# A Mamba-2 and gMLP layer on one core: the order of the first stage, two late factors, the projection weight's slots, and the last rows of the output

## The chip, the cores and the metric

The kernel runs on one core of a Trainium2 chip. The metric is the device time of one execution in microseconds (us). The core has a matrix engine (TensorE, PE in the profile; its weight loads are PEld), a vector engine (VectorE, DVE), a scalar engine (ScalarE, ACT), GpSimd (POOL) and a sync engine (SP) that here only issues loads. Each engine works through its own list of instructions in order, and semaphores make one wait for another.

## The reference

One layer, 1024 rows (time) of 1024 features, everything in fp32. Cut to what matters here:

```python
mod = silu(c) @ ada_w + ada_b
shift, scale, gate = split(mod, 3)
h = rms_norm(x, norm_w) * (1 + scale) + shift
proj = h @ w_in                 # gm_u, gm_v, gm_z, ssm_z, xbc, dt, g_a, g_b
y_a = spatial_gating(gelu(gm_u), gelu(gm_v), ...) * silu(gm_z)
y_b = rms_norm((ssd_scan(silu(conv(xbc)), dt, ...) + d_skip * xs) * silu(ssm_z), groups of 256)
merged = sigmoid(g_a) * (y_a @ w_proj_a) + sigmoid(g_b) * (y_b @ w_proj_b)
out = rms_norm(x + gate * (merged @ w_out), final_norm_w)
```

## The kernel before, in words

**Arithmetic.** A product of fp32 matrices is made of three matmuls on rounded parts: high x high, high x low, low x high. Each operand is split into them: ACT casts the high part (a CAST), DVE subtracts it to get the low part. Large products go by a Strassen scheme with seven products of half-size blocks. The normed and modulated input h is kept transposed as four blocks b11, b12, b21, b22 and their sums t1 to t4, each in four row tiles k and in a high and a low part (`b11h0`, `b11l0`, ...). One `product` is 12 matmuls of 128x512; after each one `run_tasks` moves a counter of slots on by one and runs what `later(delay, f)` has put off until that slot.

**Who sets the order.** Instructions under `pin` keep the order of the program among themselves. All others are placed by the framework's scheduler, which works with its own estimates of durations, so a task's slot decides only from when on it can be placed. Loads go to SP's queue (`load`), stores to ACT's (`store`), both in order with what else stands on the engine.

**First stage (0 to 72 us).** x is loaded in eight tiles xt[0..7]. `square(t)` sums the squares of a tile on ACT, `factors` makes the inverse root (a power on POOL), `normed` scales half a tile. Then h is made for eight blocks of 128 features in the order `KS = (0, 4, 1, 5, 2, 6, 3, 7)`; n counts the steps in this order. For step n: `matvec(n)` multiplies silu(c) with the two column blocks aw[n] of ada_w and copies the result to row; `modulation(n)` turns it to a column by two small matmuls, and two small DVE operations make md (scale and shift); `transposes(n, h)` turns half h of the rows on PE into px; `rows_of_h(n, h)` reads px with md: ACT writes the high part and an fp32 copy hf, DVE subtracts for the low part. `first_products(n)` then makes 12 matmuls of h with 256 columns of w_in (w0, split by `split_w0`) into accs, six for each half; the loop counts them with `at`, and at given counts inserts what prepares step n + 1 (`prepare`), the sums t1 to t4 (`t_first` to `t_parts`, `last_sums`) and the four matmuls of `dt_products`. `warm` issues small matmuls without use of their result. The first `vx` matmul begins the next stage.

**Pairs (148 to 920 us).** The columns of w_in in pairs of 128-column blocks, seven products each. Accumulators x and y take turns, and are emptied by ACT copies or DVE adds (`c1x`, `c2x` and so on, line 552). Beside them, from the 17th pair on, `wb_load(i)` loads each of 16 half blocks (wbr) of the second projection weight, `wb_quarter(i)` casts the fourth quadrant (wba), `wb_sums(i)` makes the sums and casts the first two parts (wbb0), and after more slots the last two (wbb2). wbr, wba and wbb have one buffer each, so a cast waits for the store of what stood there before, and a load for the last reader.

**Projection by w_proj_b (1180 to 1327 us).** Units (product name, k); in the first ones, named p1, `post2` and `post3` of the last two SSD groups are inserted: the inverse roots of their rows are turned on PE (`y3p`) and stored.

**Output (1327 to 1402 us).** Seven products by w_out in four row tiles each, added to rows of x (`collect`). The last one (a12) completes rows 0 to 3: the square of each half row is summed on ACT, `root` makes the factor, `finish` applies it and fnw (final_norm_w) and issues the store of the row. Row 3 is done in two column halves, and its factor by three Newton steps on DVE (`inv_root`).

Of the kernel before, what the change touches and what calls it, by code (L numbers as in the profile page):

```python
# [16 lines left out]
P = 128  # L17
# [4 lines left out]
NG = 8  # L22
# [13 lines left out]
def hybrid_kernel(  # L36
# [131 lines left out]
    with tc.tile_pool(name="p0", bufs=1, reuse_waits="tile") as p0:  # L168
# [65 lines left out]
        load(wd, w_in[:, COL_DT : COL_DT + NH].rearrange("(k p) c -> p k c", p=P))  # L234
        at = 0
        for src, n in [(conv_b, 32), (ssm_norm_w, 16), (gm_ln_w, 8), (gm_ln_b, 8)]:
            load(pkb[at : at + n, 0], src[0].rearrange("(r q) -> r q", q=P))
            at += n
        load(pkb[:, 1], conv_w[0].rearrange("k (i q) -> (k i) q", q=P))

        def warm(n):

            for _ in range(n):
                mm(accs[1][1][:, 0:P], ident, ones)
# [10 lines left out]
        def matvec(n):  # L255
# [7 lines left out]
            pin(V.tensor_copy(row, pm[:, 0:256]) if n == 0 else A.copy(row, pm[:, 0:256]))  # L263
# [94 lines left out]
        def halves(n):  # L358

            return (0, 1) if KS[n] < 4 else (1, 0)  # L360
# [8 lines left out]
        def factors(b):  # L369
            bs = slice(4 * b, 4 * b + 4)  # L370
# [10 lines left out]
        for t in range(4):  # L381
            square(t)
        factors(0)
        for t in range(4):
            normed(t, 0, V)
        transposes(0, 0)
        split_w0(0)
        for t in range(4):
            normed(t, 1, V)
        matvec(0)  # L390
        warm(3)
        modulation(0)
        warm(8)
        rows_of_h(0, 0)
        for t in range(4, NCH):
            square(t)
# [1490 lines left out]
```

## Time and profile before

| what | value |
|---|---|
| time, median of 3 runs | 1400.14 us (1397.68 to 1400.6) |
| the profiled execution | 1403.9 us, span of its instructions 1402.1 us |
| mean granted clock of PE | 0.991 |
| PE, DVE, ACT, POOL busy | 98%, 75%, 57%, 16% of the span |
| idle PE time in the span | 1402.1 - 1374.4 = 27.7 us |
| bytes moved | 288.60 MB, 205 GB/s over the span |

Busy shares are means over the stages. A row of the timeline or of the chain gives start, duration, engine, line and `out<-in`; what stands in brackets is the idle time of the engine before it and what ended it. A matmul row's duration reaches from the start of its first to the modelled end of its last. In a row of windows, the eighth item is the granted clock: at 0.50 PE does half its work.

### The profile page before, as it was taken

Reading aid. Unit: us, or ns where it says so; the run is one execution under the profiler, and the core shown is the slowest. Engines: PE = TensorE matmul, PEld = TensorE weight load, DVE = VectorE, ACT = ScalarE, POOL = GpSimd, SP = SyncE. Lnnn points to the kernel's source line nnn. Section 1 sums busy time; section 2 is a strip of 40 time slices with the busy share of each in tenths; the row PEclk is TensorE's granted clock in tenths of the full one; section 3 lists DMA queues with packets and bytes.
Section 4 is the critical chain, followed back from the end, with each engine's and each line's share of the span. In section 5 each row is a group of like instructions: output and inputs, shape, how many; then the busy total and the mean of one; then the engine's idle time right before and its main releaser. Section 6 shows DMA issues by size and latency. Waiting matters only on the chain.

```text
span 1402.1 us, 20253 instructions
## 1 busy us (share of the span) xinstructions
PE 1374.4 (98%) x6971; PEld 1139.7 (81%) x6971; DVE 1045.4 (75%) x1703; ACT 802.2 (57%) x1448; POOL 220.0 (16%) x208
## 2 busy tenths in 40 slices
PE   8999999999999999999999999999999999999997
PEld 6688878888888888887888888888888878888886
DVE  3777766777778889777788686388767755859976
ACT  5764656666566665555676555587766714233443
POOL 0000000000000011200200100027878750000001
PEclk9999999999999999999999999999999999999999
DMA  8675443343334668686675774498777748978913
GB/s 265 191 239 149 120 120 108 110 128 106 131 110 146 200 195 267 210 259 213 191 219 180 226 229 134 160 350 310 279 253 278 272 152 289 333 252 316 379 44 120
DMA packets 247227, 288.60 MB, mean 206 GB/s; under 512 B 14508, under 2 KB 194132, under 8 KB 247124
## 3 DMA queue, kind: packets, MB, share of 16 engines
q1 hardware_dynamic: 173716, 203.76, 45.3%
q10 hardware_dynamic: 73408, 83.54, 17.5%
q8 instruction: 55, 0.90, 0.3%
q14 instruction: 48, 0.39, 0.1%
HBM read 199.79 MB, written 87.46 MB: 205 GB/s over the span
## 4 chain that ended last, share of the span: by engine, by line
PE 77%; DMA 11%; DVE 5%; ACT 2%; issue 2%; POOL 1%; SPq 1%; ACTq 0%; DVEq 0%; POOLq 0%
PE xcb L536 6%; PE xuz L536 6%; PE xz L536 6%; PE xx L536 6%; PE xg L536 5%; PE vx L921 3%; PE yz L536 3%; PE ycb L536 3%; PE yuz L536 3%; PE yx L536 3%; PE yg L536 3%; PE pma L81 3%; DMA dcy<-acs_d 2%; PE ox L1750 2%; PE oy L1750 2%
## 5 line engine op out<-in xcount | busy, mean ns | idle before, releaser
L759 POOL TENSOR_TENSOR wog<-wog,gb 128x256 f32<-128x256 f32 x16 | 23.0, 1454 | 626.4 <-DMA wog<-in_w_out_dram 587.7
L1079 ACT ACTIVATE dcy<-dcy,nacs 128x128 f32<-128x128 f32 x256 | 78.5, 389 | 14.7 <-POOL dcy L1074 14.6
L1074 POOL TENSOR_SCALAR_AFFINE_SELECT dcy<-dcy 128x1024 f32<-128x1024 f32 x32 | 34.9, 1091 | 142.6 <-DMA yl<-ya_d 96.1
L1071 ACT ACTIVATE ea<-dcy 64x512 f32<-64x512 f32 x64 | 40.0, 626 | 14.5 <-DMA dcy<-acs_d 11.9
L81 PE MATMUL pma<-yh,wah 128*128 128x512 f32 x128 | 44.4, 428 | 0.0
L994 ACT ACTIVATE ac<-ac 128x1024 f32<-128x1024 f32 x32 | 33.9, 1061 | 16.4 <-DVE ac L992 16.2
L81 PE MATMUL pma<-yh,wal 128*128 128x512 f32 x128 | 43.0, 417 | 0.0
L1099 DVE TENSOR_TENSOR dcy<-dcy,pc 128x1024 f32<-128x1024 f32 x32 | 39.0, 1218 | 5.1 <-PE pc L84 4.2
L1159 DVE TENSOR_TENSOR ym<-yn,ea 128x512 f32<-128x512 f32 (+1 forms) x32 | 19.9, 623 | 30.2 <-PE yn L81 30.1
L1496 DVE SCALAR_TENSOR_TENSOR yn<-yn,par,rb 128x512 f32<-128x512 f32 x32 | 24.0, 749 | 23.8 <-DMA yn<-yb_d 23.8
L1161 POOL TENSOR_TENSOR yz<-y,sl 128x512 f32<-128x512 f32 x32 | 41.3, 1291 | 1.1
L81 PE MATMUL pma<-yl,wah 128*128 128x512 f32 x128 | 40.9, 402 | 0.0
L1160 POOL TENSOR_TENSOR y<-y,ym 128x512 f32<-128x512 f32 (+1 forms) x32 | 36.5, 1141 | 14.5 <-DVE ym L1159 14.1
L791 ACT CAST wbb<-wbr 128x512 fp32r<-128x512 f32 x32 | 19.8, 619 | 32.6 <-DMA wb_d<-wbb 25.6
L81 PEld LDWEIGHTS yn<-sl,st 128*128 128x128 f32 x224 | 30.5, 191 | 8.5 <-POOL yz L1181 2.3
L81 PE MATMUL sp<-xe,bn 128*128 128x256 f32 x112 | 33.6, 418 | 3.2 <-DVE ssq L1190 1.8
L81 PE MATMUL yn<-sl,st 128*128 128x128 f32 x224 | 31.5, 277 | 5.1 <-DVE st L1129 5.1
L992 DVE SCALAR_TENSOR_TENSOR ac<-c2cb,cwt,ac 128x1023 f32<-128x1023 f32 (+2 forms) x24 | 31.1, 1296 | 6.7 <-ACT ac L990 6.6
L81 PE MATMUL yi<-dcy,xd 128*64 128x128 f32 x512 | 35.4, 281 | 0.1
L992 DVE SCALAR_TENSOR_TENSOR ac<-c2x,cwt,ac 128x1023 f32<-128x1023 f32 (+2 forms) x24 | 30.7, 1280 | 5.9 <-ACT ac L990 5.8
L1765 POOL TENSOR_TENSOR r<-r,fnw 128x512 f32<-128x512 f32 x2 | 2.5, 1293 | 205.9 <-ACT junk L1763 205.9
L1127 POOL TENSOR_TENSOR st<-st,cd 128x256 f32<-128x256 f32 x48 | 32.8, 684 | 10.8 <-PE yn L81 8.2
(2982 smaller groups left out, 4440.4 us busy)
## 6 DMA issues: line engine op xcount, KB each, us to landing
sl<-s_d SPq DMA_DIRECT2D x32, 768.0 KB
s_d<-ac ACTq DMA_DIRECT2D x32, 512.0 KB
wb_d<-wbb ACTq DMA_DIRECT2D x32, 512.0 KB
dcy<-acs_d SPq DMA_DIRECT2D x32, 512.0 KB
av<-in_w_in_dram SPq DMA_DIRECT2D x36, 256.0 KB
aw<-in_ada_w_dram SPq DMA_DIRECT2D x16, 512.0 KB
wbr<-in_w_proj_b_dram SPq DMA_DIRECT2D x32, 256.0 KB
yb_d<-yz ACTq DMA_DIRECT2D x32, 256.0 KB
```

The lines of the kernel that those rows point to most:

```text
L81: pin(PE.matmul(acc, l, r, start=first, stop=last))
L536: pin(PE.matmul(ps, lw[:, k * P : (k + 1) * P], r[k], start=first and n + k == 0, stop=n == 2 and k == 3, skip_group_check=not first))
L921: pin(PE.matmul(ps[pn][j], l[:, j * P : (j + 1) * P], r, start=nm in ("p1", "p5", "p2") and n + units[i][1] == 0, stop=n == 2 and k == 3, ...
L992: V.scalar_tensor_tensor(ac[:, s:], cc[:, : S - s], conv_wt[:, 3 - s, i : i + 1], ac[:, s:], op0=ALU.mult, op1=ALU.add)
L994: A.activation(ac, ac, AF.Silu)
L1071: A.activation(ea[hh * HD : (hh + 1) * HD], dcy.rearrange("p (j e) i l -> p e j (i l)", e=2)[hh * HD : (hh + 1) * HD, hh], AF.Exp)
L1074: G.affine_select(out=d8, in_=d8, compare_op=ALU.is_ge, fill=-1e30, base=0, pattern=[[0, 2 * HPG], [1, P]], channel_multiplier=-1)
L1079: A.activation(dcy[:, h, i, :], dcy[:, h, i, :], AF.Exp, bias=sub[:, i, h : h + 1])
L1099: V.tensor_tensor(d3, d3, pc[:, 0:256].unsqueeze(1).to_broadcast([P, HPG, 256]), op=ALU.mult)
L1160: G.tensor_add(y1[:, :, t0:], y1[:, :, t0:], m[:, :, t0:])
L1161: G.tensor_mul(yz, y1, sl[:, 4:6])
L1750: pin(PE.matmul(ps, a[:, tsl], b[:, cs], start=first and n + j == 0, stop=n == 2 and j == 3, skip_group_check=not first))
```

## The change

Four parts.

1. **First stage.** The factors of a half are made in two steps (three tiles, then one; `squares`). All `normed` are on DVE (two tiles were on ACT), and the copy of row 0 is on ACT. Step 0 is written out by hand: the transposes of step 1's first half go early, the `warm` matmuls are 16 instead of 22 after the first split and go into pd, step 0 is begun with six products, then come matvec(1), the transposes and rows for its second half, modulation(1), and step 1's first half between the remaining products. In `prepare`, matvec stands together with one half's transposes at place 2, and modulation with the other half's at place 7, followed by both `rows_of_h`; before, the four stood at 1, 3, 5 and 9. Some sums and `dt_products` are at later places. The loads of wd and of the small parameters come after those of aw[2] and w0[2].
2. **Weight halves.** Loads come every 9 slots instead of 43 // 5, the quarter 4 slots after the load instead of 2, and the last two parts 2 slots after the first two instead of 3.
3. **Last factors.** The two `post3` are at k = 4 and 6 of p1 instead of 3 and 4.
4. **End.** All instructions of the last product are pinned in a written order. Rows 0 to 3 are each finished in halves: ACT on the high columns (POOL has multiplied those by fnw), DVE on the low ones. Row 3's factor is a power on POOL.

```diff
-            pin(V.tensor_copy(row, pm[:, 0:256]) if n == 0 else A.copy(row, pm[:, 0:256]))
+            pin(A.copy(row, pm[:, 0:256]))
...
-            return (0, 1) if KS[n] < 4 else (1, 0)
+            return (0, 1) if KS[n] < 4 or n == 1 else (1, 0)
...
+        def squares(a, b):
+            for t in range(a, b):
+                square(t)
+            factors(a, b)
+
+        squares(0, 3)
+        squares(3, 4)
+        for half in range(2):
+            for t in range(4):
+                normed(t, half, V)
         transposes(0, 0)
         split_w0(0)
-        for t in range(4):
+        matvec(0)
+        load_aw(2)
+        load_w0(2)
+        late_loads()
+        transposes(1, 0)
+        warm(2)
+        modulation(0)
+        rows_of_h(0, 0)
+        squares(4, 7)
+        for t in (4, 5):
+            normed(t, 0, V)
+        squares(7, 8)
+        for t in (6, 7):
+            normed(t, 0, V)
+        warm(8)
+        start = first_products(0)
+        for _ in range(6):
+            next(start)
+        warm(6)
+        matvec(1)
+        for t in (4, 5):
             normed(t, 1, V)
-        matvec(0)
-        warm(3)
-        modulation(0)
-        warm(8)
-        rows_of_h(0, 0)
-        for t in range(4, NCH):
-            square(t)
-        factors(1)
-        for half in range(2):
-            for t in range(4, NCH):
-                normed(t, half, A if t > 5 else V)
+        transposes(0, 1)
+        modulation(1)
+        rows_of_h(0, 1)
         split_w0(1)
+        for t in (6, 7):
+            normed(t, 1, V)
+        for _ in range(4):
+            next(start)
+        rows_of_h(1, 0)
+        for _ in start:
+            pass
 
         def prepare(n):
 
-            if n == 1:
+            a, b = halves(n)
+            if n == 2:
                 return {
-                    6: lambda: (warm(6), transposes(0, 1), rows_of_h(0, 1), matvec(1), warm(5)),
-                    8: lambda: (transposes(1, 1), modulation(1), rows_of_h(1, 1)),
-                    12: lambda: (transposes(1, 0), rows_of_h(1, 0)),
+                    4: lambda: (transposes(1, 1), rows_of_h(1, 1), matvec(n)),
+                    8: lambda: (transposes(n, a), modulation(n), transposes(n, b), rows_of_h(n, a), rows_of_h(n, b)),
                 }
-            a, b = halves(n)
             return {
-                1: lambda: matvec(n),
-                3: lambda: transposes(n, a),
-                5: lambda: (modulation(n), rows_of_h(n, a)),
-                9: lambda: (transposes(n, b), rows_of_h(n, b)),
+                2: lambda: (matvec(n), transposes(n, a)),
+                7: lambda: (modulation(n), transposes(n, b), rows_of_h(n, a), rows_of_h(n, b)),
             }
...
-            sums[2 * k + 1, 4] = [(dt_products, k)]
+            sums[2 * k + 1, (8, 2, 2, 8)[k]] = [(dt_products, k)]
...
-        later(3, wb_parts, i, "wbb", 2, 2, raw[:, 0:2])
+        later(2, wb_parts, i, "wbb", 2, 2, raw[:, 0:2])
...
-                    later(43 * i // 5, wb_load, i)
-                later(2 + 43 * i // 5, wb_quarter, i)
+                    later(9 * i, wb_load, i)
+                later(4 + 9 * i, wb_quarter, i)
...
-        if nm == "p1" and k in (3, 4):
-            groups[NG - 5 + k].post3()
+        if nm == "p1" and k in (4, 6):
+            groups[NG - 4 + k // 2].post3()
...
-            if c and t in (2, 3):
+            if c and t < 4:
                 G.tensor_mul(r[:, cs], r[:, cs], fnw[:, cs])
...
-        if t == 2:
-            A.mul(r[:, 512:1024], r[:, 512:1024], y)
-            V.scalar_tensor_tensor(r[:, 0:512], r[:, 0:512], y, fnw[:, 0:512], op0=ALU.mult, op1=ALU.mult)
+        if t < 4:
+            pin(A.mul(r[:, 512:1024], r[:, 512:1024], y))
+            pin(V.scalar_tensor_tensor(r[:, 0:512], r[:, 0:512], y, fnw[:, 0:512], op0=ALU.mult, op1=ALU.mult))
...
+    finish(1, y1)
+    last_add(3, acc["x"][3][:, 0:256], lo, dde[:, 32:33])
+    y2 = root(2)
+    pin(G.tensor_mul(r[:, lo], r[:, lo], fnw[:, lo]))
+    pin(V.scalar_tensor_tensor(dde[:, 33:34], dde[:, 32:33], D * EPS, part[:, 11:12], op0=ALU.add, op1=ALU.add))
+    last_add(3, acc["y"][3][:, 0:256], hi, part[:, 3:4])
+    finish(2, y2)
+    v, y = dde[:, 34:35], dde[:, 35:36]
+    pin(V.tensor_scalar(v, part[:, 3:4], dde[:, 33:34], 1.0 / D, op0=ALU.add, op1=ALU.mult))
+    pin(G.tensor_tensor(y, v, nhalf[:, 0:1], op=ALU.pow))
+    pin(A.mul(r[:, 512:1024], r[:, 512:1024], y))
+    nc.scalar.dma_start(out[3 * P : 4 * P, 512:1024], r[:, 512:1024])
```

What this does to the order of instructions shows at three places. The first is VectorE in step n = 2 of the first stage, from the low part of b11's row tile 1 to md3, the scale and shift of step 3 (names end in a number of the buffer). Before:

```order
L301 TENSOR_TENSOR b11l1_159<-hf1_497,b11h1_155 128x512
L324 TENSOR_TENSOR hf4_439<-hf4_439 128x512
L307 TENSOR_TENSOR t3l0_190<-hf0_233,t3h0_186 128x512
L301 TENSOR_TENSOR b12_1_513<-hf1_497,b12_1_513 128x512
L307 TENSOR_TENSOR t2l0_174<-hf4_439,t2h0_170 128x512
L221 TENSOR_TENSOR w0l3_461<-w0r3_459,w0h3_460 128x256
L272 TENSOR_TENSOR md3_554<-pm3_530,par_138 128x1
```

And now:

```order
L303 TENSOR_TENSOR b11l1_159<-hf1_499,b11h1_155 128x512
L320 TENSOR_TENSOR hf0_233<-hf4_439,hf0_233 128x512
L303 TENSOR_TENSOR b12_1_503<-hf1_499,b12_1_503 128x512
L321 TENSOR_TENSOR hf4_439<-hf4_439,hf0_233 128x512
L309 TENSOR_TENSOR t1l0_166<-hf0_233,t1h0_162 128x512
L309 TENSOR_TENSOR t3l0_190<-hf0_233,t3h0_186 128x512
L326 TENSOR_TENSOR hf4_439<-hf4_439 128x512
L221 TENSOR_TENSOR w0l3_451<-w0r3_449,w0h3_450 128x256
L309 TENSOR_TENSOR t2l0_174<-hf4_439,t2h0_170 128x512
L274 TENSOR_TENSOR md3_557<-pm3_529,par_138 128x1
```

The second sums of hf0 and hf4 and the low part of t1 now stand between b11l1 and md3 too: eight operations of 128x512 instead of five.

The second place is ScalarE in the pairs, between the cast of half 6's last parts (wbb2_6), which is the last to read wbr6, and the first cast of half 7 (wba4_7). Before:

```order
L791 CAST wbb2_6_5655<-wbr6_5504 128x2x256
L552 COPY c1z2_5489<-xz2_5474 128x512
L93 DMA wb_d3_108<-wbb2_6_5655 128x4x256
L522 CAST p2x5h_5462<-a12x5_5437 128x512
L522 CAST p7x5h_5466<-a21x5_5433 128x512
L791 CAST wba4_7_5741<-wbr7_5703 128x256
```

And now, from the store of wbb2_6 on (between that cast and this store stands one cast, p2x5h):

```order
L93 DMA wb_d3_108<-wbb2_6_5718 128x4x256
L545 CAST p7x5h_5452<-a21x5_5419 128x512
L1023 ACTIVATE c1z2_5481<-c1z2_5481 128x1024
L545 CAST p4x5h_5456<-a22x5_5421 128x512
L93 DMA s_d2_115<-c1z2_5481 512x1x256
L575 COPY c2z2_5582<-xz2_5460 128x512
L545 CAST p1g6h_5600<-a11g6_5585 128x512
L575 COPY c1x5_5641<-xx5_5628 128x512
L545 CAST p5g6h_5604<-s1g6_5593 128x512
L575 COPY p5x5_5658<-yx5_5643 128x512
L93 DMA wo_d2_101<-wog4_5695 128x3x256
L545 CAST p6g6h_5608<-s2g6_5594 128x512
```

The next row is the cast of wba4_7. Ten operations of ScalarE stand ahead of it instead of three.

The third place is the end of VectorE's list. Here dde and dthq hold the sums and factors, r0 to r3 are rows, ox3 and oy3 the accumulators of row 3's halves. Before:

```order
L1843 TENSOR_TENSOR r3_12403<-r3_12403,ox3_12444 128x256
L1773 SCALAR_TENSOR_TENSOR r1_12358<-r1_12358,dde_147,fnw_12528 128x1024
L1779 TENSOR_TENSOR dde_147<-dthq_146 128x1
L1847 SCALAR_TENSOR_TENSOR dde_147<-dde_147,dthq_146 128x1
L1843 TENSOR_TENSOR r3_12403<-r3_12403,oy3_12448 128x256
L1780 TENSOR_SCALAR dde_147<-dde_147 128x1
L1731 TENSOR_SCALAR dde_147<-dthq_146,dde_147 128x1
L1771 SCALAR_TENSOR_TENSOR r2_12387<-r2_12387,dde_147,fnw_12528 128x512
```

And now:

```order
L1788 SCALAR_TENSOR_TENSOR r1_12356<-r1_12356,dde_147,fnw_12526 128x512
L1856 TENSOR_TENSOR r3_12401<-r3_12401,ox3_12442 128x256
L1796 TENSOR_TENSOR dde_147<-dthq_146 128x1
L1797 TENSOR_SCALAR dde_147<-dde_147 128x1
L1878 SCALAR_TENSOR_TENSOR dde_147<-dde_147,dthq_146 128x1
L1856 TENSOR_TENSOR r3_12401<-r3_12401,oy3_12446 128x256
L1788 SCALAR_TENSOR_TENSOR r2_12385<-r2_12385,dde_147,fnw_12526 128x512
L1882 TENSOR_SCALAR dde_147<-dthq_146,dde_147 128x1
L1886 SCALAR_TENSOR_TENSOR r3_12401<-r3_12401,dde_147,fnw_12526 128x256
```

Row 1's scaling is half as wide and stands ahead of both adds of row 3; before, its full width stood between them. The eight small Newton operations that followed row 2's scaling are gone.

More of the change, by code (lines that the diff above doesn't have):

```diff
@@ L437, in hybrid_kernel @@
         for k in range(4):
-            sums[2 * k + 1, 4] = [(dt_products, k)]
-        for n in range(KT):
+            sums[2 * k + 1, (8, 2, 2, 8)[k]] = [(dt_products, k)]
+        for n in range(1, KT):
             todo = prepare(n + 1) if n + 1 < KT else {}
@@ L1822, in hybrid_kernel @@
             continue
+        if nm == "a12":
+            break
         for t in range(4):
[L1824 to L1825 removed]
             for j in range(4):
@@ L1837, in hybrid_kernel, with last_add @@
                 finish(4 + t, y4[:, t : t + 1])
[L1838 to L1840 removed]
+    def last_add(t, ps, cs, total):
+        r = rows[t]
+        pin(V.tensor_add(r[:, cs], r[:, cs], ps))
+        pin(A.activation(junk[:, cs], r[:, cs], AF.Square, accum_out=total))
+    lo, hi = slice(0, 256), slice(256, 512)
+    ps, r = acc["y"], rows[3]
+    for t in range(3):
+        for j in range(4):
+            out_products(ps[t], "a12", "b21", j, t, whole, True)
+        last_add(t, ps[t], whole, part[:, t : t + 1])
+        if t == 1:
+            finish(0, y0)
+        if t == 0:
+            y0 = root(0)
+        elif t == 1:
+            y1 = root(1)
+    for m, cs in enumerate((lo, hi)):
         for j in range(4):
             out_products(acc["xy"[m]][3][:, 0:256], "a12", "b21", j, 3, cs, True)
[L1843 to L1849 removed]
+    finish(1, y1)
[7 more added lines that the diff above has]
+    pin(V.tensor_scalar(v, part[:, 3:4], dde[:, 33:34], 1.0 / D, op0=ALU.add, op1=ALU.mult))
+    pin(G.tensor_tensor(y, v, nhalf[:, 0:1], op=ALU.pow))
+    pin(A.mul(r[:, 512:1024], r[:, 512:1024], y))
+    nc.scalar.dma_start(out[3 * P : 4 * P, 512:1024], r[:, 512:1024])
+    pin(V.scalar_tensor_tensor(r[:, hi], r[:, hi], y, fnw[:, hi], op0=ALU.mult, op1=ALU.mult))
+    pin(V.tensor_scalar_mul(r[:, lo], r[:, lo], y))
     nc.sync.dma_start(out[3 * P : 4 * P, 0:512], r[:, 0:512])
[L1851 to L1852 removed]
     ps3.__exit__(None, None, None)
```

71 lines of the change are left out of this document (22 added, 49 removed).

## The prediction

> **What bounds the kernel now.** I read the page's first two parts, then what TensorE (PE) waited for, then the windows around each wait, then the chain of waits at both ends.
>
> ```profile
> PE 1374.4 (98%) x6971; PEld 1139.7 (81%) x6971; DVE 1045.4 (75%) x1703; ACT 802.2 (57%) x1448; POOL 220.0 (16%) x208
> PE xx L536 <- ACT c2x L552: 2.0, 1, 2.0
> PE y3p L84 <- POOL ssq L1194: 0.3, 1, 0.3
> ```
>
> PE is busy 1374.4 of 1402.1 us, and the change leaves the number of its large products alone. So it can only win or lose in PE's 27.7 idle us, in the time PE runs at a lower clock, and after the last matmul. Idle time on another engine counts only where a PE wait follows it. The second number of a wait row is how often, the last the longest.
>
> The windows (span, busy time and count of PE, PEld, DVE, ACT, POOL, granted clock, DMA share, GB/s) show what a wait costs beyond itself:
>
> ```profile
> 649.64:653.05 3.41, 1.36 (x6) 1.05 (x6) 3.41 (x7) 3.11 (x6) 0.00 (x0) 1.00 0.27 90
> 653.05:656.47 3.42, 3.42 (x9) 2.67 (x8) 3.42 (x5) 1.10 (x2) 0.00 (x0) 0.50 0.71 229
> 21.59:25.00 3.41, 2.01 (x17) 1.14 (x20) 1.84 (x5) 2.08 (x4) 1.02 (x1) 1.00 0.58 126
> 25.00:28.41 3.41, 3.41 (x23) 2.52 (x16) 1.12 (x2) 2.38 (x5) 0.00 (x0) 0.50 1.05 300
> ```
>
> A window of 3.41 us with 1.36 or 2.01 us of PE work is followed by one at clock 0.50, which does half its work: 3.42 x 0.5 = 1.71 us lost. So the wait on c2x costs 2.05 + 1.71 = 3.76 us. The page "TensorE: Matmul & The Clock Gate" of the Trainium skill (Part 1) puts the half clock after at least one idle window of about 3.4 us; by it this wait, shorter than that, would cost 2.05 us alone and my sum would end 1.7 us higher. The rows contradict it: the first window was 40% busy and the half clock followed.
>
> **The change, part by part.** Times are measured against the profiled execution: span 1402.1 us, its own time 1403.9, that is 3.8 above the median 1400.14 of the runs shown.
>
> *A, first stage.* These rows are PE's in before, from the timeline and (the last seven) the chain of waits:
>
> ```profile
> 23.46 1.18 PE L84 MATMUL px<-ident,x 128*128 128x128 f32 x4 [1.32 <-DMA pkb<-in_ssm_norm_w_dram]
> 24.57 1.60 PE L81 MATMUL pm<-aw,scz 128*32 128x256 f32 x16
> 28.26 0.77 PE L81 MATMUL acc<-b,w0h 128*128 128x512 f32 x2
> 31.12 0.49 PE L81 MATMUL acc<-b22h,w0h 128*128 128x512 f32 x1
> 39.12 0.66 PE acc L81 x2
> 40.22 0.46 PE acc L81 x2
> 41.02 1.04 PE acc L81 x4
> 42.49 0.93 PE acc L81 x4
> 58.09 0.99 PE pd L81 x8
> 68.50 1.67 PE pd L81 x8
> ```
>
> Start: the six products of n = 0, half 0, come earlier, but PE then stands at matvec(1) until aw1 is in, 24.57 at the latest, where the old matvec starts without a wait. From there: matvec 1.60 to 26.1 or 26.2, four transposes at most 1.1 (23.46 to 24.57), to 27.2, the first row of h on ACT 0.78 (a row below) to 28.0, half 1's six products to 29.6 at most (0.46 each at half clock until 28.4, then 0.23). If aw1 is in a us sooner, n = 1 starts at 28.5. I take 29.1 against 31.12: -2.0 (-2.7 to -0.5; the small end if the longer wait brings a second window at half clock).
>
> Fewer breaks: two products after a lone matvec took 0.66 instead of 0.46, four after a lone modulation 1.04 instead of 0.93. matvec and modulation now stand next to transposes; half of these 0.31 us in each of six steps: -0.9 (-1.9 to 0). dt_products of n = 7 took 1.67 instead of 0.99 because its hf was late; it moves from place 4 to 8, and the four products before it (0.9 us) are more than that: -0.7.
>
> Against it: modulation moves from place 5 to 7 and md is DVE work behind a backlog. Durations of before around md3:
>
> ```profile
> 37.75 0.69 DVE L301 TENSOR_TENSOR b11l<-hf,b11h 128x512 fp32r<-128x512 f32 x1
> 38.36 0.68 DVE L324 TENSOR_TENSOR hf<-hf 128x512 f32<-128x512 f32 x1
> 40.77 0.42 DVE L221 TENSOR_TENSOR w0l<-w0r,w0h 128x256 fp32r<-128x256 f32 x1
> 41.10 0.15 DVE L272 TENSOR_TENSOR md<-pm,par 128x1 f32<-128x1 f32 x1
> 41.47 0.78 ACT L297 ACTIVATE b22h<-px,md 128x512 fp32r<-128x512 f32 x1 [0.36 <-DVE md L273]
> 43.03 0.39 PE L81 MATMUL acc<-b22h,w0h 128*128 128x512 f32 x1
> ```
>
> A 128x512 DVE operation takes a pitch of 0.61 (38.36 - 37.75). Five of them and the w0l stood from b11l to md3 (3.35 us); now eight and the w0l, 8 x 0.61 + 0.33 = 5.2. md3 was done at 41.4, b22h's first result at 42.25, PE wanted it at 43.03: slack 0.78 us. The backlog eats 1.85 of it, but b11l starts perhaps 0.5 earlier in the step, and PE reaches n = 3 about 0.1 sooner: a wait of 0.4 to 1.4, I take 1.0. The same holds ahead of n = 4 and n = 6, where t1, t3 and t2 of ACT also stand ahead of the rows of h: 3 x 1.0. At n = 7 (b22's low part) 0.5 and at vx, whose operand waits behind the late t1, 0.6. Sum of the losses 4.1 (1.5 to 6.0).
>
> A = -2.0 - 0.9 - 0.7 + 4.1 = **+0.5**, bounds -2 to +3.5. The moved loads (aw2 and w0r2 ahead of wd and pkb on SP) cost nothing: wd is now used at place 8 and pkb at place 12.
>
> *B, halves of the projection weight.* ACT and SP around the c2x wait, ACT's waits, and one product of 12 matmuls from the chain:
>
> ```profile
> 638.77 2.29 SPq L90 DMA_DIRECT2D wbr<-in_w_proj_b_dram  x2
> 646.23 0.41 ACT L791 CAST wba<-wbr 128x256 fp32r<-128x256 f32 x1 [4.66 <-DMA wbr<-in_w_proj_b_dram]
> 649.00 1.24 ACT L990 ACTIVATE ac<-c1x,par,cwt 128x1024 f32<-128x1024 f32 x1 [1.84 <-DVE c1x L552]
> 651.17 0.57 ACT L552 COPY c2x<-xx 128x512 f32<-128x512 f32 x1
> ACT wba L791 <- DMA wbr<-in_w_proj_b_dram: 24.3, 11, 4.7
> ACT wbb L791 <- DMA wb_d<-wbb: 25.6, 15, 3.0
> 656.28 2.88 PE xg L536 x12
> ```
>
> The load of half 7 is issued at 638.77, since its buffer is released late, and the cast of wba that needs it stands so early in ACT's order that ACT stops for 4.66 us; behind it queue the casts, ac and the copy of c2x for which PE waits. All 11 such waits total 24.3 us, yet only this one reaches PE. Now ten ACT operations instead of three lie between the cast that releases the buffer and this one. Seven more at 0.57 (the copy) and one of them near 1.24 (ac) are 4.7 us, just what is wanted; a rest of it is hidden by the slack named next: **-3.8**.
>
> What is late next: the second wbb part comes two slots after the first instead of three, a slot being one product, 2.88 us. Its tile is free only when the store of the first has landed. ACT's wait there was 1.7 on average (25.6 / 15) and 3.00 at most, without any PE wait; one slot less makes it up to 4 or 5. An accumulator that ACT empties is wanted again two products later, 5.8 us, less a copy of 0.57. So mostly hidden; unhidden it costs 1 to 3.8. B: -3.8 to 0; above that see the rivals.
>
> *C, post3 of the last two factors.* The y3p wait goes. The last factor's turn moves by two units of the projection and its user comes some four units later: **-0.3** (+1 if its store is late then).
>
> *D, the end.*
>
> ```profile
> 1392.22 1.28 DVE L1773 SCALAR_TENSOR_TENSOR r<-r,dde,fnw 128x1024 f32<-128x1024 f32 x1
> 1393.01 0.28 PE L1750 MATMUL oy<-mwhb,ma11h 128*128 128x256 f32 x1
> 1393.42 0.68 DVE L1779 TENSOR_TENSOR dde<-dthq 128x1 f32<-128x1 f32 x1
> 1394.10 0.41 DVE L1843 TENSOR_TENSOR r<-r,oy 128x256 f32<-128x256 f32 x1
> 1394.60 0.42 ACT L1844 ACTIVATE junk<-r 128x256 f32<-128x256 f32 x1 [1.68 <-DVE dde L1780]
> 1394.64 0.54 POOL L1781 TENSOR_TENSOR dde<-dde,nhalf 128x1 f32<-128x1 f32 x1 [0.56 <-DVE dde L1780]
> 1395.14 0.21 DVE L1731 TENSOR_SCALAR dde<-dthq,dde 128x1 f32<-128x1 f32 x1 [0.57 <-ACT junk L1844]
> 1395.27 1.19 DVE L1771 SCALAR_TENSOR_TENSOR r<-r,dde,fnw 128x512 f32<-128x512 f32 x1
> 1397.96 0.72 ACT L1851 ACTIVATE r<-r,dde 128x512 f32<-128x512 f32 x1 [2.02 <-DVE dde L1743]
> 1398.71 0.40 ACTq L1852 DMA_DIRECT2D out_dram<-r  x1
> ```
>
> Before: the last matmul ends at 1393.3, the 1.28 of r1 and the 0.68 hold r3's add until 1394.10; after the square r2's 1.19 and six small operations hold ACT's last product until 1397.96. After: add at about 1393.5 (0.41), square to 1394.5, scalar step 0.21, POOL's power 0.54 to 1395.5, ACT 0.72 from 1395.6: 2.4 earlier. r2's 512 KB are issued just ahead of r3's and share the queues, so I take **-1.9** (-2.4 to -1.0). POOL now also multiplies rows r0 and r1 by fnw. "SBUF — State Buffer" of the Trainium skill (two separate sides) says that a DVE operation with two SBUF inputs and a GpSimd one lock each other out for a whole instruction; by that page the sum could lose a further 0.7. The rows agree in kind (0.68 for a 128x1 add, started while POOL worked), and do not show how often it hits.
>
> **The rivals.**
> 1. *Forecast*: +0.5 - 3.8 - 0.3 - 1.9 = -5.5: 1403.9 to 1398.4 by the profiled execution, 1394.6 from the median. The phase of the 3.41 us windows can differ from run to run, so the median run may hold fewer half-clock stretches than the profiled one (it is 3.8 shorter); I take 0.6 less gain: **1395.2**, own range 1391.5 to 1398.5.
> 2. *B's wait is only exchanged*: ACT waits for the store instead and PE still loses 3.8 once: -1.7, **1398.4**. For it: 15 store waits already and one slot less. Against: none of them reached PE.
> 3. *Slower*: the store wait reaches PE in several halves. Place: ACT's second wbb cast. It decides where the wait and the ACT work queued behind it exceed 5.8 - 0.57 = 5.2 us. Where PE then loses 1.4 us, a window is down to the 2.01 us of the row above, and 1.71 of half clock follow, 3.1 together. With three of the 16 halves: +9.3 - 3.8 + 0.5 - 0.3 - 1.9 = +3.8, **1403.9**; with two 1400.8. Against: the largest wait of 3.00 left PE untouched.
> 4. *Late modulation lowers the clock*: each of the three md waits of 1.0 becomes 1.4 and brings 1.71 more: +0.5 + 3 x 2.1 = +6.8 for A, sum +0.8, **1400.9**. For it: 2.01 us busy did it; against: 1.4 must fall into one window, which runs free.
> 5. *The end brings nothing*, because the last row's transfer waits behind r2's: -3.6, 1396.5; inside the forecast's range.
>
> **How the numbers follow.** Chances: forecast with rival 5 0.60, exchange 0.15, slower 0.15, modulation 0.10. The measurement can tell 0.2%, 2.8 us, from no change: 1397.3 to 1402.9. Faster: 0.57 of the forecast and 0.04 of the exchange, 0.61. Same: 0.03 + 0.11 + 0.08 = 0.22. Slower: 0.15 + 0.02 = 0.17. The range goes from 1391.0, a little under the forecast's own lower end (0.03 left out), to 1402.0, which takes in the exchange and most of the modulation case and leaves out the slower one (0.16 with the rest). Cases of both signs hold most of the chance, so the forecast's own range stands above.
>
> **What would show it.** Right: no PE wait on c2x near 650 and no window at clock 0.50 there; ACT's waits on wbr for wba far below 24.3 us; n = 1 starting at 29 to 29.5; waits of about 1 us of PE on b22h or b11h ahead of n = 3, 4 and 6; vx starting at 72 to 73; the last output DMA issued about 2 us sooner after the last matmul than 5.4 us. Wrong: a new PE wait behind a copy that queues after wbb; half-clock windows in the first stage after 30 us; vx later than 75 or earlier than 70.

## The result, and the profile after

The change makes no difference that can be measured: 1401.17 us median against 1401.19 (14 runs of each). The ratio is 0.9999 with a 95% interval of 0.9983 to 1.0016, which is -2.4 to +2.2 us. The forecast was 1395.2 us, and faster. The profiled execution after took 1400.27 us, its span is 1398.5.

These are the first part of the page and, of what TensorE waited for, the rows that bear on the change, after:

```profile
PE 1366.6 (98%) x6959; PEld 1131.6 (81%) x6959; DVE 1047.8 (75%) x1701; ACT 800.1 (57%) x1447; POOL 221.7 (16%) x212
PE pm L81 <- DMA aw<-in_ada_w_dram: 3.1, 2, 2.9
PE x0p L1581 <- DVE p6bl L1557: 1.7, 2, 1.3
PE acc L81 <- ACT b11h L299: 1.5, 2, 0.7
PE xcb L559 <- ACT c2cb L575: 1.1, 1, 1.1
PE xg L559 <- ACT c1g L575: 1.0, 1, 1.0
PE vx L944 <- ACT p1v0h L874: 0.8, 1, 0.8
PE acc L81 <- ACT b22h L299: 0.6, 1, 0.6
```

The wait on c2x (2.0 us) is gone, as the change wants, but there are waits at other points that before did not have. A new wait can be looked for where a matmul starts late, so the starts of the same matmuls in the two traces are the best map (us; the last column is after minus before):

```text
matmul                                         before    after     diff
first vx (end of the first stage)               72.06     73.86    +1.80
xuz behind the wait on c1uz                    187.4     187.7     +0.34
xx, 5 us on                                    192.3     191.0     -1.27
xg behind the wait on c1g                      603.4     605.0     +1.61
xg behind the wait on c2x of before            656.1     654.1     -2.01
pma, end of the SSD stage                     1133.9    1130.4     -3.55
x0p, ahead of the waits on p6bl               1177.4    1173.0     -4.37
x0p, behind them                              1218.6    1217.0     -1.61
last matmul                                   1393.01   1391.63    -1.37
end of the span                               1402.1    1398.5     -3.6
```

This pair of traces says -3.6 us, the 14 runs of each say nothing. The difference is the clock. Windows of before and of the experiment e4, whose instructions are the same up to the last product:

```profile
185.43:188.84 3.41, 1.57 (x7) 1.21 (x7) 3.38 (x6) 3.41 (x8) 0.00 (x0) 1.00 0.01 2
188.84:192.25 3.41, 3.41 (x9) 2.64 (x9) 3.36 (x5) 2.54 (x4) 0.00 (x0) 0.50 0.45 154
```

```profile
185.40:192.25 6.85, 6.85 (x32) 5.63 (x31) 6.57 (x11) 4.59 (x7) 0.00 (x0) 1.00 0.26 82
649.00:655.90 6.90, 6.90 (x32) 5.69 (x31) 5.05 (x7) 4.75 (x7) 0.00 (x0) 1.00 0.77 222
1124.00:1134.30 10.30, 10.11 (x79) 8.38 (x79) 6.43 (x12) 0.37 (x1) 7.08 (x8) 1.00 0.15 53
```

The trace of before holds 20.5 us at half clock ahead of the last matmul, that of the changed kernel 6.8, that of e4 none. The first pair differs by 13.7 x 0.5 = 6.8 us from that alone, more than the -3.6. The trace of before, on which the prediction rests, is an extreme one: its mean clock is 0.991, and the 111 runs of before that were made beside the experiments had 0.993 to 0.999. Below, times therefore come from the repeated runs, and traces tell waits and places.

### The profile page after: what moved, and what is told of

The parts are those of the page before. It is cut to its first block, busy times and chain, and to the rows that moved or that the text cites. A ratio compares the mean times of both kernels' runs of the same rounds, so it can differ in the third digit from the quotient of the medians.

```text
span 1398.5 us, 20239 instructions
## 1 busy us (share of the span) xinstructions
PE 1366.6 (98%) x6959; PEld 1131.6 (81%) x6959; DVE 1047.8 (75%) x1701; ACT 800.1 (57%) x1447; POOL 221.7 (16%) x212
## 4 chain that ended last, share of the span: by engine, by line
PE 77%; DMA 8%; DVE 7%; ACT 3%; issue 3%; POOL 2%; SPq 1%; ACTq 0%; DVEq 0%; POOLq 0%
PE xuz L559 6%; PE xx L559 6%; PE xcb L559 5%; PE xz L559 5%; PE xg L559 4%; PE pma L81 3%; PE ox L1767 3%; DMA dcy<-acs_d 3%; PE yuz L559 3%; PE yp L1581 3%; PE vx L944 3%; PE yx L559 3%; PE ycb L559 3%; PE yz L559 3%; PE yg L559 2%
## 5 line engine op out<-in xcount | busy, mean ns | idle before, releaser
L1782 POOL TENSOR_TENSOR r<-r,fnw 128x512 f32<-128x512 f32 x4 | 5.3, 1345 | 204.5 <-ACT junk L1780 204.5
L979 ACT ACTIVATE vm<-vm,vr 128x128 f32<-128x128 f32 x64 | 25.8, 483 | 16.2 <-DMA vm<-v_d 15.8
```

## The experiments

Each ratio is to the kernel before on the same chip, with its 95% interval (8 to 12 runs of each version, 23 to 34 of before).

| run | what it is | ratio | interval |
|---|---|---|---|
| e1_first_stage | only the first stage | 1.0044 | 1.0025 to 1.0063 |
| e2_halves | only the halves | 0.9993 | 0.9979 to 1.0008 |
| e3_factors | only the factors' turns | 1.0009 | 0.9995 to 1.0022 |
| e4_end | only the end | 0.9992 | 0.9974 to 1.0010 |
| e5_no_factors | all but the factors' turns | 1.0034 | 1.0019 to 1.0050 |
| e10_old_first_stage | all but the first stage | 0.9984 | 0.9970 to 0.9998 |
| e8_modulation_5 | all, modulation at place 5 | 1.0017 | 1.0002 to 1.0032 |
| e6_halves_three | halves, last parts three slots on | 0.9995 | 0.9980 to 1.0010 |
| e7_halves_end | e6 and the end | 0.9974 | 0.9960 to 0.9988 |
| e9_quarter_end | only the quarter later, and the end | 0.9984 | 0.9970 to 0.9998 |
| e11_gated_earlier | e7, wog 3 slots earlier | 0.9976 | 0.9961 to 0.9990 |
| e12_gated_later | e7, wog 3 slots later | 0.9975 | 0.9961 to 0.9989 |

**One part each.** The edit of e1 to e4 is in each the hunks of one part of the change, the other hunks left out.

e1_first_stage:

```diff
+        squares(0, 3)
...
+                2: lambda: (matvec(n), transposes(n, a)),
+                7: lambda: (modulation(n), transposes(n, b), rows_of_h(n, a), rows_of_h(n, b)),
```

> Only the new first stage; halves, factors and end as before. Theory (the loss in the first stage is given back at the next wait that does not depend on the matrix engine): vx starts about 1.8 us later than before (near 73.9 us), the wait on c1uz near 185 us shrinks from 1.8 to about 0 and no half-clock window follows it, so that from 190 us on the kernel is level with before or up to 1.6 us ahead; time within 0.2% of before. Rival (a delay of the matrix engine at the start is carried to the end): the c1uz wait stays at 1.8 us and the span grows by 1.8 to 2.2 us.

It was 0.44% slower, some 6 us, which neither theory gave. vx starts at 72.31 us against 70.64 and 70.84 in e3 and e4, which have the old stage, like it without a half-clock window there: 1.5 to 1.7 us late. The wait on c1uz was 0.2 us, as the theory has it, but e2, e4, e10 and e12 have it at 0.3 to 0.5 with the old stage, so that shows nothing. The rest of the loss lies elsewhere. TensorE's waits in e1, and two windows:

```profile
PE y3p L84 <- POOL ssq L1217: 3.1, 1, 3.1
PE y2p L84 <- POOL ssq L1217: 1.4, 1, 1.4
```

```profile
1172.70:1176.10 3.40, 0.93 (x5) 0.43 (x3) 0.92 (x3) 0.00 (x0) 1.08 (x1) 1.00 0.96 385
1176.10:1179.50 3.40, 2.78 (x8) 2.21 (x9) 2.34 (x5) 0.62 (x1) 0.56 (x1) 0.50 0.08 24
```

A change of the first 72 us makes TensorE wait 4.5 us between 1169 and 1177 us, and a half-clock window follows. The order explains where it comes from. Apart from the first stage and a swap of two operations near 95 us, VectorE's list is that of before up to 1161 us, and then differs around these two waits. There the program's scheduler puts a scaling of yn, a normed operand of the projection, ahead of ssq, the sums of which POOL makes the roots for y2p and y3p. VectorE in the first units of the projection, left before, right e1 (sums of p1a and a scaling left out; _0 and _1 are the two halves of a row tile):

```text
SCALAR_TENSOR_TENSOR yn_0<-yn_0,par,rb_0          TENSOR_TENSOR p1bl<-yn_0,p1bh
TENSOR_TENSOR p1bl<-yn_0,p1bh                     SCALAR_TENSOR_TENSOR yn_1<-yn_1,par,rb_1
                                                  TENSOR_TENSOR p1bl<-yn_0,p1bh
TENSOR_SCALAR ssq<-y0p                            TENSOR_SCALAR ssq<-y0p
```

The chain of waits in e1 runs through just such a scaling and its load. Rows of it:

```profile
1166.64 7.39 DMA yn<-yb_d
1174.12 0.75 DVE yn L1519
1174.87 0.08 DVE ssq L1213
1174.95 0.07 issue
1175.02 1.65 POOL ssq L1217
```

Counted from the first x0p matmul of the projection, y0p's ssq starts 9.1 us on in before, behind eight scalings, and 14.2 us on in e1, behind nine. Nine also stand ahead of it in the changed kernel (12.2 us) and in e5 (13.4 us). In every other run there are eight, and 8.7 to 9.4 us.

e2_halves:

```diff
-        later(3, wb_parts, i, "wbb", 2, 2, raw[:, 0:2])
+        later(2, wb_parts, i, "wbb", 2, 2, raw[:, 0:2])
...
-                    later(43 * i // 5, wb_load, i)
-                later(2 + 43 * i // 5, wb_quarter, i)
+                    later(9 * i, wb_load, i)
+                later(4 + 9 * i, wb_quarter, i)
```

> Only the weight halves' slots. Theory (an exchange): the wait on c2x near 650 us is gone (-2.1 us, -3.7 with its half-clock window), and two new waits of about 1.0 to 1.2 us each stand near 592 us (xcb for c2cb) and 603 us (xg for c1g), behind casts of wbb that wait for the store; net 0 to -1.6 us, time within 0.2%. Rival (the new waits come from the later first stage, not from the slots): no new waits near 592 and 603 us and a gain of 2.1 to 3.7 us.

The exchange is there with the old first stage too: no wait on c2x, 1.7 us on c2cb and 1.0 us on c1g. The rival falls. That casts of wbb cause it, as the theory has it, this run does not show.

e3_factors:

```diff
-        if nm == "p1" and k in (3, 4):
-            groups[NG - 5 + k].post3()
+        if nm == "p1" and k in (4, 6):
+            groups[NG - 4 + k // 2].post3()
```

> Only the last two factors' turns. Theory (the later store of the last factor holds SyncE's loads of rb and yn, and the vector engine then has a backlog): a new wait of TensorE on p6bl near 1210 to 1220 us, 1.7 to 2.8 us in all, and the y3p wait of 0.3 gone; the kernel 1.5 to 2.5 us slower. Rival (in the changed kernel TensorE came 4 us sooner to a stretch that the vector engine bounds, whatever the turns are): no wait on p6bl here, the time 0 to 0.3 us below before.

Between the two: 0.09% slower, an interval that includes no change, and waits of 1.3 us on tri and 0.4 us on p6bl in place of y3p's 0.3. (VectorE copies the turned root y3p into tri, and p6bl is the low part of an operand; TensorE can go on in both cases only when VectorE is done.)

e4_end:

```diff
+    last_add(3, acc["y"][3][:, 0:256], hi, part[:, 3:4])
+    finish(2, y2)
...
+    pin(G.tensor_tensor(y, v, nhalf[:, 0:1], op=ALU.pow))
```

> Only the end by hand. Theory (the chain after the last matmul is shorter by itself): from the start of the last matmul to the end of the span 6.9 us instead of 9.1, all else as before; -2.2 us, 0.16%. Rival (the transfer of the last rows or the pinned order costs it back): 8 to 9 us after the last matmul, or waits of TensorE in the last product, and no gain.

From the start of the last matmul to the end it takes 6.96 us instead of 9.14. The -0.08% of the repeated runs agrees with 2.2 us, and with nothing.

**Parts left out.** e5_no_factors is the changed kernel with this hunk undone:

```diff
-        if nm == "p1" and k in (4, 6):
-            groups[NG - 4 + k // 2].post3()
+        if nm == "p1" and k in (3, 4):
+            groups[NG - 5 + k].post3()
```

> The changed kernel with the last two factors' turns as before (k = 3 and 4). Theory (the new first stage makes the scheduler put one more yn scaling ahead of the two sums that post3 needs, so that early turns wait; the later turns are the answer to that and cost a smaller wait on p6bl): the waits y2p and y3p on POOL's ssq come back, 3 to 4.5 us together, the wait on p6bl of 1.7 us is gone; 1 to 4 us slower than the changed kernel, 0.1 to 0.4% slower than before. Rival (the later turns are a plain loss of 2.7 us): no y2p or y3p wait above 0.5 us, 2 to 3 us faster than the changed kernel.

The theory holds: 0.34% slower than before, where the whole change is level, and TensorE waits again on POOL, with nothing of 0.2 us or more on p6bl:

```profile
PE y3p L84 <- POOL ssq L1217: 3.0, 1, 3.0
PE y2p L84 <- POOL ssq L1217: 0.6, 1, 0.6
```

So inside the change the later turns are an answer to what the new first stage does to the order. By themselves they cost waits (1.7 us in e3), and whether time too e3 leaves open.

e10_old_first_stage is the changed kernel with all hunks of the first stage undone:

```diff
-                2: lambda: (matvec(n), transposes(n, a)),
-                7: lambda: (modulation(n), transposes(n, b), rows_of_h(n, a), rows_of_h(n, b)),
+                1: lambda: matvec(n),
+                3: lambda: transposes(n, a),
+                5: lambda: (modulation(n), rows_of_h(n, a)),
+                9: lambda: (transposes(n, b), rows_of_h(n, b)),
```

> The changed kernel with the first stage of before. Theory (within the change the new first stage costs its 1.7 us at vx and what it does to the order of the projection): vx starts at 70.6 to 72.1 us, 1.5 to 5 us faster than the changed kernel, 0.1 to 0.3% faster than before; the later factors' turns still cost a wait on p6bl or tri of 0.5 to 2 us. Rival (the loss of the first stage is wholly taken up by the waits behind it, so that the parts around it decide): the same as the changed kernel within 1 us.

It is 0.16% faster than before, with vx at 70.45, a little under the range given, and waits of 1.3 us on tri and 0.4 on p6bl. That speaks for a cost of the first stage of some 2 us inside the change, but its interval and the whole change's overlap, so the size stays open.

**The late modulation.** e8_modulation_5, against the changed kernel:

```diff
-                7: lambda: (modulation(n), transposes(n, b), rows_of_h(n, a), rows_of_h(n, b)),
+                5: lambda: (modulation(n), rows_of_h(n, a)),
+                7: lambda: (transposes(n, b), rows_of_h(n, b)),
```

> The changed kernel with modulation and the first rows of h back at place 5 in steps 3 to 7, matvec with the transposes still at 2 and the second half's transposes at 7. Theory (the late modulation behind the vector engine's backlog causes the waits on b22h and b11h of 0.65, 0.75 and 0.74 us): these waits fall below 0.3 us each and vx starts 1.5 to 2.2 us sooner than in the changed kernel. Rival (the backlog itself, the sums moved together, causes them wherever the modulation stands): the waits stay within 0.2 us and vx starts within 0.5 us of the changed kernel, leaving half-clock windows aside.

The theory holds. The waits of the changed kernel, and what is left in e8:

```profile
42.77 0.73 PE L81 MATMUL acc<-b22h,w0h 128*128 128x512 f32 x2 [0.65 <-ACT b22h L299]
50.18 0.73 PE L81 MATMUL acc<-b11h,w0h 128*128 128x512 f32 x2 [0.75 <-ACT b11h L299]
63.21 0.73 PE L81 MATMUL acc<-b11h,w0h 128*128 128x512 f32 x2 [0.74 <-ACT b11h L299]
73.86 0.73 PE L944 MATMUL vx<-p1v0h,b11h 128*128 128x512 f32 x2 [0.81 <-ACT p1v0h L874]
```

```profile
55.36 1.07 PE L81 MATMUL pm<-aw,scz 128*32 128x256 f32 x16 [0.36 <-DVE cwt L448]
64.51 0.61 PE L81 MATMUL pm<-ones,row 128*128 128x1 f32 x4 [0.35 <-ACT row L265]
72.07 0.72 PE L945 MATMUL vx<-p1v0h,b11h 128*128 128x512 f32 x2 [0.79 <-ACT p1v0h L875]
```

vx starts 1.8 us sooner, both traces having one half-clock window there. The total does not follow: 0.17% slower than before. In the traces the lead goes on the way. From 580 to 1000 us e8 is only 0.1 to 0.3 us ahead of the changed kernel, after two waits that this has not, 0.5 us on c1g and 0.6 on p5cb. At 1105 us, in the SSD stage, it is 1.3 us behind. At the projection y3p waits 2.3 us for tri, and a half-clock window follows, where the changed kernel waits 1.7 us on p6bl; at 1225 us e8 is 2.8 us behind.

One more thing is to be learned from e8. In it only eight scalings stand ahead of y0p's ssq, as in before, and y0p's ssq starts 9.2 us after the first x0p. e8 differs from the changed kernel by the place of modulation and one half's rows alone, so the scheduler's choice 1100 us later hangs on that place, and not on the new first stage as a whole. e8 keeps the later turns, which have nothing to answer there; a run of it with the early turns was not made.

**The halves, taken apart.** e6_halves_three keeps three slots, e7_halves_end adds the end:

```diff
-        later(2, wb_parts, i, "wbb", 2, 2, raw[:, 0:2])
+        later(3, wb_parts, i, "wbb", 2, 2, raw[:, 0:2])
```

> The kernel before with halves every 9 slots and the quarter 4 slots after the load, but the last two parts 3 slots after the first two, as before. Theory (the two new waits near 592 and 603 us come from ACT waiting for the store of wbb with one slot less): neither is there, the c2x wait near 650 us stays away, 2 us less than before, up to 3.7 where no half-clock window follows; 0.15 to 0.25% faster. Rival (any spacing of nine slots puts a cast ahead of a copy somewhere): one or two waits of 1 us or more on a copy by ACT between 460 and 860 us, time within 0.1% of before.

> As e6_halves_three with the end by hand; first stage and factors as before. Theory: the gains add up, 2 us and 2.2 us, 0.2 to 0.4% faster than before, and 6.9 us from the last matmul's start to the end. Rival (what is gained ahead of the SSD stage is lost there in a wait for the vector engine or a transfer): last matmul at the same time as before within 1 us, once half-clock windows are taken off, and 0.15% at most.

With three slots the wait on c1g is still 1.0 us (c2cb 0.3 in e6, 1.0 in e7): the rival's case. So the slot less is not what makes them. It may add to c2cb's, which is 0.9 to 1.7 us in the five traces with two slots; c1g's near 604 us is 0.9 or 1.0 in all seven. e7 has the lowest ratio and its gain is clear: 0.26%, 0.12 to 0.40%, as its theory has it; the 0.15% of its rival lies just inside the interval.

In the changed kernel these are the two waits, and what ACT, VectorE and POOL do around them:

```profile
592.82 1.19 PE L559 MATMUL xcb<-t4h,p4cb5h 128*128 128x512 f32 x4 [1.08 <-ACT c2cb L575]
604.96 1.19 PE L559 MATMUL xg<-t3h,p7g4h 128*128 128x512 f32 x4 [0.96 <-ACT c1g L575]
```

```profile
586.94 0.37 ACTq L93 DMA_DIRECT2D wo_d<-wog  x1
587.35 0.41 ACT L814 CAST wba<-wbr 128x256 fp32r<-128x256 f32 x1 [5.73 <-DVE wog L793]
597.94 2.31 DVE L1015 SCALAR_TENSOR_TENSOR ac<-c1cb,cwt,ac 128x1021 f32<-128x1021 f32 x1
592.60 4.87 POOL L782 TENSOR_TENSOR wog<-wog,gb 128x256 f32<-128x256 f32 x2 [23.41 <-DMA wog<-in_w_out_dram]
```

ACT stands 5.73 us until the store of wog can be issued, for which VectorE's sums of wog were late, and behind that store stand the cast of the half, the convolution's first step and the copy of c2cb. Then POOL's two multiplications take 4.87 us instead of 2.54 (before, at 587.93), while a step of VectorE's convolution takes 2.31 instead of 1.27. Both stretches have to do with wog, the gated output weight, whose tasks come every 11 slots. e9, e11 and e12 move the one series against the other. e9_quarter_end, against before (with the end by hand):

```diff
-                later(2 + 43 * i // 5, wb_quarter, i)
+                later(4 + 43 * i // 5, wb_quarter, i)
```

> The kernel before with the end by hand, and of the halves' change only the quarter 4 slots after the load instead of 2 (loads every 43 // 5 slots, last parts 3 slots on, as before). Theory (the c2x wait goes because the cast of wba comes later, and the waits of 1 us on c2cb and c1g near 592 and 603 us come from the shifted loads, which bring a half's sums on the vector engine into its backlog there): no wait on c2x, none above 0.5 us on c2cb or c1g, 0.25 to 0.4% faster than before. Rival (later quarters alone bring the same backlog): waits of about 1 us on copies by ACT somewhere between 460 and 860 us, gain 0.15 to 0.3% like the halves with three slots and the end.

The theory fell in half: c2cb and c1g do not wait, but the wait on c2x stays, with 1.8 us and a half-clock window at 650.3. The later quarter alone does not remove it; with the loads' new slots as well, in e6, it is gone. (The loads of before come at slot 43 * i // 5, every 8.6 slots on the average.)

e11_gated_earlier, against e7 (e12_gated_later has 13 in place of the 7):

```diff
-            later(10 + 11 * i + 33 * (i > 5), gated_weights, gb, i)
+            later(7 + 11 * i + 33 * (i > 5), gated_weights, gb, i)
```

> As e7_halves_end, with the gated output weights (wog) started 3 slots earlier. Theory (the waits on c2cb and c1g of 1 us each come from the halves' sums and casts falling together with GpSimd's multiplications of wog and the sums and store of wog, which slow or hold the vector and the scalar engine): both waits below 0.3 us, c2x still gone, 1 to 2 us less than e7_halves_end. Rival (any place of wog collides with some half): one or two waits of about 1 us on other copies by ACT between 460 and 860 us, time as e7_halves_end within 1 us.

> As e7_halves_end, with the gated output weights started 3 slots later. Theory as for the earlier start: the waits on c2cb and c1g near 592 and 604 us change in size or place with wog, since the halves stand where they stood. Rival (the halves and the convolution alone make the vector engine's backlog): both waits as in e7_halves_end within 0.3 us.

TensorE's waits between 75 and 920 us, first e11, then the two longest of e12 (two of 0.3 us, on c1uz and c1z, follow):

```profile
PE xuz L536 <- ACT c1uz L552: 1.8, 1, 1.8
PE xg L536 <- ACT c2g L552: 0.2, 1, 0.2
```

```profile
PE xx L536 <- ACT c1x L552: 1.9, 2, 1.1
PE xcb L536 <- ACT c2cb L552: 1.1, 1, 1.1
```

Three slots earlier, both waits are gone, and c2x's too. Three slots later, c1g's is gone, c2cb's stays and c1x waits 1.9. So the place of wog beside the halves decides c1g's wait, as the theory says. c2cb's varies too much between traces of the same instructions (0.3 in e6, 1.0 in e7) for one trace each to decide it. Which of wog's effects does it is not settled: in e11 POOL's pair still takes 5.61 us and the convolution 2.30, without a wait of TensorE. Nor did 2 us less of waits show: e7, e11 and e12 are alike within their intervals.

## Why the prediction was wrong

Two steps of the sum failed. Part A was added up as far as vx only, and part B took the waits that come in place of c2x's for mostly hidden. The parts in turn:

**The first stage, +0.5.** Sign right, size wrong, and its main effect missed. Step by step, e3's trace (old stage) and the changed kernel's, us from the first product of step n to that of the next, the last to vx:

```text
n              1      2      3      4      5      6      7
old          6.60   5.30   6.51   5.82   6.49   5.58   4.64
new          6.89   6.01   7.41   5.45   7.58   5.32   5.33
```

The steps grew by 3.0 us in all, in e1 and e5 too. By kind, a matmul counted to the start of the next and waits apart, us for the seven steps:

```text
        waits   products   dt_products   transposes   matvec and other     all
old      0.00      23.58          4.65         4.25               8.45   40.93
new      2.94      22.86          3.98         5.89               8.32   43.99
```

The waits are a little under the 4.1 forecast, and the three of 0.65 to 0.75 stand at b22h and b11h, where the prediction put them; at n = 7 there is none. The -0.7 for dt_products came (two of the four moved to place 8, two to place 2), and of the -0.9 for fewer breaks the products brought 0.7. What the sum left out are the transposes, +1.6: 0.5 for four of step 1 that stood ahead of its start before, and 1.1 because the twelve other sets of four took 0.45 us each instead of 0.36. That looks as if the breaks had moved to the transposes instead of going; no run tests it.

The start brought -1.25 (29.87 against 31.12) instead of -2.0. matvec(1) began at 24.05, sooner than the 24.57 allowed for, and though it ran at half clock the high part of half 1 was ready at 27.85, where the prediction had 28.0. Its path left out the low part:

```profile
24.05 1.93 PE L81 MATMUL pm<-aw,scz 128*32 128x256 f32 x16 [2.90 <-DMA aw<-in_ada_w_dram]
27.75 0.77 ACT L299 ACTIVATE hf<-px,md 128x512 f32<-128x512 f32 x1
28.55 0.69 DVE L303 TENSOR_TENSOR b<-hf,b 128x512 fp32r<-128x512 f32 x1 [0.77 <-ACT hf L299]
29.30 0.73 PE L81 MATMUL acc<-b,w0h 128*128 128x512 f32 x2 [0.19 <-DVE b L303]
```

ACT makes the fp32 copy hf only behind the high part, VectorE subtracts from it, and the last two of the six products cannot start before 29.30. The six took 1.97 us instead of 1.6.

So vx came 1.8 us late instead of 0.5, which is inside the bounds given. The larger error is that the sum ended at vx. The order 1100 us later changed with the first stage, and e1 and e5 show 3.6 to 4.5 us of waits from that; no step of the prediction looked there. Alone the first stage costs 0.44%, some 6 us.

**The halves, -3.8.** The wait on c2x went. Its windows at the same place, after:

```profile
649.00:652.41 3.41, 3.41 (x17) 2.83 (x16) 2.58 (x4) 1.62 (x3) 0.00 (x0) 1.00 0.49 140
652.41:655.82 3.41, 3.41 (x16) 2.83 (x16) 1.77 (x2) 2.31 (x4) 0.00 (x0) 1.00 0.27 77
```

The failed step is "mostly hidden": 2.0 us came back at c2cb and c1g, the exchange that was the second rival with 0.15. That rival named the store of wbb as its mechanism, and e6 shows that three slots do not remove the waits; e11 and e12 show, for c1g's, the place of wog beside the halves instead. And 1.71 of the 3.8 is a half-clock window that not every execution has: of the five traces with a wait on c2x (before, e1, e3, e4 and e9; 1.3 to 2.2 us), only before and e9 have one behind it. The 0.6 taken off for that was too little. Alone the halves bring 0.07%, 1 us, and not 3.8.

**The factors, -0.3.** Wrong in sign by the waits: 1.7 us in place of 0.3, in e3 as in the changed kernel. The slack of "some four units" is not there, because SyncE's loads are in order. Its list after, then before:

```profile
1180.76 0.32 SPq L90 DMA_DIRECT2D p3a<-wb_d  x1
1187.05 0.32 SPq L90 DMA_DIRECT2D rb<-rs_d  x1
1187.42 0.43 SPq L90 DMA_DIRECT2D yn<-yb_d  x1
```

```profile
1183.40 0.32 SPq L90 DMA_DIRECT2D p3a<-wb_d  x1
1183.82 0.48 SPq L90 DMA_DIRECT2D rb<-rs_d  x1
1184.36 0.59 SPq L90 DMA_DIRECT2D yn<-yb_d  x1
```

The load of rb waits for the last factor's store, and the loads of yn wait behind it: 6.3 us without a load instead of 0.4. VectorE then stands 5.67 us for yn:

```profile
1192.72 0.75 DVE L1519 SCALAR_TENSOR_TENSOR yn<-yn,par,rb 128x512 f32<-128x512 f32 x1 [5.67 <-DMA yn<-yb_d]
```

From there VectorE has a backlog, and TensorE falls back 2.8 us against before (-4.37 to -1.61 in the table of starts). Inside the change this is still the smaller evil, as e5 shows: with the early turns it is 0.34% slower than before, with the late ones level.

**The end, -1.9.** Right, 2.2 us. The chain after, to be held against the rows of before:

```profile
1391.63 0.28 PE L1767 MATMUL oy<-mwhb,ma11h 128*128 128x256 f32 x1
1391.95 0.42 DVE L1856 TENSOR_TENSOR r<-r,oy 128x256 f32<-128x256 f32 x1 [0.16 <-PE oy L1767]
1393.25 0.54 POOL L1883 TENSOR_TENSOR dde<-dde,nhalf 128x1 f32<-128x1 f32 x1 [0.75 <-DVE dde L1882]
1393.83 0.72 ACT L1884 ACTIVATE r<-r,dde 128x512 f32<-128x512 f32 x1 [0.30 <-POOL dde L1883]
1394.58 0.41 ACTq L1885 DMA_DIRECT2D out_dram<-r  x1
```

The add starts 0.32 us after the last matmul's start (1.09 before), the output's store 2.95 (5.70 before). The output's store is issued 2.75 us sooner and the end comes 2.2 us sooner, so the rival in which the last row's transfer waits behind r2's took at most half a us.

**The rivals.** The slower case did not come: no wait after the halves reached 1.4 us within one window, and no half-clock window follows them. Late modulation lowering the clock did not come either: its waits are 0.65 to 0.75. What came in its place is a case without a rival: parts whose worth depends on one another. Alone they sum to +0.44 - 0.07 + 0.09 - 0.08 = +0.38%, together they are -0.01%. The later turns show it best: alone +0.09%, inside the change -0.35% (0.9999 against e5's 1.0034), for there they take back most of what the first stage loses at the projection.

## What to carry to other kernels

Where a scheduler places the instructions, compare the order of every engine over the whole program, also far behind the edited stage, and look for an operation that now stands ahead of one that somebody waits for. Two series of tasks with periods of 9 and 11 slots meet somewhere; cost a new period at the place where they meet, not at the wait that it removes. A single trace that differs by 0.2% may differ by its clock alone: count the time at half clock first, and take the time from repeated runs.

## What was not expected of the hardware

The same instructions up to the last product ran with 20.5 us at half clock ahead of the last matmul in one execution, of before, and with none in another, of e4 (span up to the last matmul 1393.0 and 1384.2 us). The wait on c1uz, with no edit near it, was 0.3 to 2.1 us in the runs with the old first stage. And VectorE and POOL were both slower where they worked at the same time, more than the prediction allowed for: a convolution step went from 1.27 to 2.31 us, a pair of multiplications from 2.54 to 4.87. That agrees with the page "SBUF — State Buffer" of the Trainium skill (two separate sides), by which a VectorE operation with two SBUF inputs and a GpSimd one that reads SBUF lock each other out; the prediction had weighed it at the end of the kernel only.
